# Reading the moving tile of a matmul from its two halves in turn, in a transformer block on one core

## The chip, the cores and the metric

The kernel runs on one core of a Trainium2 chip. The metric is the device time of one execution in microseconds, the median of several runs. Each kernel also has one profiled execution, from which all profile lines here come; its own time is given beside its span (first to last instruction of the program).

## The reference

One layer of a hybrid block on a sequence of 256 tokens of width 4096, all in float32. Cut to what matters, it is a chain of large products with attention-like work between them:

```python
h = _rmsnorm(x, norm_w[layer])
u = h @ w_in[layer]                                   # 4096 x 15424
... # split u: queries, keys, values and gates of an mLSTM (8 heads)
... # and of a sparse attention with three branches (16 heads)
y_ml = hm.reshape(B, S, ML_WIDTH) * jax.nn.sigmoid(ml_o) * jax.nn.silu(ml_z)
y_ns = _nsa(...) * jax.nn.silu(ns_z)
x = x + jnp.concatenate([y_ml, y_ns], axis=-1) @ w_out[layer]         # 4096 x 4096
x = x + jax.nn.sigmoid(x @ ple_gate[layer]) * (p[layer] @ ple_proj[layer])   # 4096 x 4096, 256 x 4096
```

The weights are some 400 MB of float32 and each is used once. With 256 tokens, each 128x512 piece of weights is multiplied by two stationary blocks of 128 tokens.

## The kernel before

**One product.** The activations are stationary (128 channels x 128 tokens, tiles `sh` and `sl`), the weights are the moving operand (128 channels x 512 output columns), and the result is a 128 x 512 accumulator in PSUM. To keep accuracy each float32 operand is split in a high and a low float32r part: ScalarE writes `whi` as a rounded copy of the loaded tile `raw` (line 1479), VectorE writes `wlo = raw - whi` (line 1480). A product is then three matmuls: high by high, low activations by high weights, high activations by low weights (function `product`, line 1234).

**Units.** The program is written out as a list of units. Each takes one tile `raw` of 128 x 2 x 512 (512 KB, one transfer from the SP queue), two blocks of 128 channels by 512 columns. `wide_group` (from line 894) makes eight groups of 16 units: each unit has 12 matmuls, on lines 913 and 915. `pair_group` makes all larger groups, 1024 columns each. Its plain units (`c_unit`) have 12 matmuls; its mixed units use a scheme with seven products in place of eight for a 2 x 2 arrangement of blocks, for which VectorE adds blocks of weights (function `sums`, lines 1277 to 1281) and of activations (tiles `cb`). All matmuls of `pair_group` are issued by `emit`, on line 1192. `p_unit` (lines 1373 to 1375) multiplies the small projection `ple_proj` in four of the groups.

Some products are not of this kind: `small_group` (lines 985, 986) has the weights as stationary operand and activations of 256 columns as the moving one, also float32r; `cmp_unit` (line 1005) takes plain float32 tiles; the two attentions (lines 539 to 631 and 707 to 733) multiply activations with activations.

**Order.** Engines work in the order that the loop at the end of `hymba_block` writes out. For each unit `n` it emits the split of unit `n + LOOK`, loads as long as fewer than six tiles are held, the unit's matmuls, and then a step of the other work (evictions, attention) from queues of generators:

```python
LOOK = 3
RAWB = 6
...
        if n + LOOK < N and not late:
            split(n + LOOK)
...
        load_some()
...
        un["mm"](*splits.pop(n))
```

So ScalarE and VectorE run up to three units ahead of TensorE, in four buffers each of `whi` and `wlo`.

**Layout.** The host function `_layout` lays the weights out so that each transfer is one contiguous piece of DRAM: `_blocks` for the groups of 512 columns and `ple_proj`, `_pairs` for the groups of 1024. In a tile, the 512 columns of a block are neighbours in a partition, 2 KB long.

Of the kernel before, what the change touches and what calls it, by code (L numbers as in the profile page):

```python
# [87 lines left out]
def hymba_block(ctx: ExitStack, tc: tile.TileContext, a, out: bass.AP):  # L88
    nc = tc.nc
    MM = nc.tensor.matmul  # L90
# [9 lines left out]
    def bank(bset, i, shape):  # L100
        if bset:
            return side(i, shape)
        return psp.tile(shape, F32, tag=f"mm{i // 2}", name=f"mm{i // 2}", bufs=2)
# [97 lines left out]
    def require(flag):  # L201
        n = 0
        while flag not in done:
            n += 1
            assert (step() or step_dry()) and n < 10000, flag
# [556 lines left out]
    sh, sl = [None] * 8, [None] * 8  # L762
# [125 lines left out]
    def gemm_unit(src, mm, pre=None, post=None, kind="wide"):  # L888
        units.append(dict(src=src, mm=mm, pre=pre, post=post, kind=kind))
# [4 lines left out]
    def wide_group(name, w, stat_flag, post, marks=None, after=None):  # L894

        flag = f"ev_{name}"
        box = {}
        prev = evq[-2] if len(evq) >= 2 else None
        evq.append(flag)

        def start():
            if prev:
                require(prev)
            box["ps"] = [bank(0, 2 - 2 * (SINGLES.index(name) % 2), [128, 512]) for _ in range(2)]

        for u in range(16):
            def mm(hi, lo, u=u):
                for j in range(2):
                    c, k = divmod(2 * u + j, 4)
                    first, last = (u == 0 and j == 0), (u == 15 and j == 1)  # L910
                    for s, m, st in ((sh, hi, first), (sl, hi, False)):
                        for t in range(2):
                            MM(box["ps"][t], s[c][:, k, t * 128:(t + 1) * 128], m[:, j, :], start=st, stop=False)  # L913
                    for t in range(2):
                        MM(box["ps"][t], sh[c][:, k, t * 128:(t + 1) * 128], lo[:, j, :], start=False, stop=last)  # L915

            def pre(u=u):
                if u == 0:
                    start()
                if stat_flag and u % 2 == 0:  # L920
                    require(f"{stat_flag}{u // 2}")

            def fin(u=u):
                if marks and u % 2:
                    done.add(f"{marks}{u // 2}")
                if u == 15:
                    post(box["ps"], flag)

            gemm_unit(w[u], mm, pre, fin)
            if after:  # L930
                after(u)
# [233 lines left out]
    def t_gate_own(g, own, us):  # L1165
# [9 lines left out]
        for j in range(2):  # L1175
# [11 lines left out]
                nc.vector.tensor_tensor(y[:, :, c0:c0 + 512], y[:, :, c0:c0 + 512], u, op=OP.mult)  # L1187
            yield

    def emit(seq):  # L1190
        for acc, s, m in seq:
            MM(acc.t, s, m, start=acc.i == 0, stop=acc.i == acc.n - 1)  # L1192
            acc.i += 1

    def pair_group(g, w, stat):
# [36 lines left out]
            return lambda k, t: (sh[c][:, b + k, t * 128:(t + 1) * 128], sl[c][:, b + k, t * 128:(t + 1) * 128])  # L1232

        def product(acc, st, hi, lo):
            return [(acc, st[0], hi), (acc, st[1], hi), (acc, st[0], lo)]

        def both(*products):
            emit([p for ps in zip(*products) for p in ps])
# [53 lines left out]
        def c_unit(kp, k, last):  # L1292
            split = split_and_sum

            def mm(hi, lo):
                bl = blocks(kp)
                if last:

                    tail.append((bl, k, hi, lo))
                    if len(tail) < (4 if g == 7 else 2):  # L1300
                        return
                    if g < -6:
                        for j in range(2):
                            for bl, k_, hi, lo in tail:
                                both(*(product(own[t][j], bl(k_, t), hi[:, j], lo[:, j]) for t in range(2)))
                        return
                    order = [(t, j) for j in range(2) for t in range(2)]
                    seq = [(b, i) for b in order[0:2] for i in range(3)] + [(b, 3) for b in order[0:2]]
                    for (t, j), i in seq + [(b, i) for b in order[2:4] for i in range(4)]:
                        bl, k_, hi, lo = tail[i]  # L1310
                        emit(product(own[t][j], bl(k_, t), hi[:, j], lo[:, j]))
                    return
                for j in range(2):
                    both(*(product(own[t][j], bl(k, t), hi[:, j], lo[:, j]) for t in range(2)))

            def post():
                if k:
                    finish(kp)
            unit(w[kp, k], split, mm, kp, post=post)

        def a_units(kp):
            def split1(r):
                raw[kp] = [r]
                return split_one(r)

            def split2(r):
                raw[kp].append(r)
                opened.extend(((kp, 0), (kp, 1)))
                return split_all(r, keep=True)

            def mm1(hi, lo):
                emit(product(oth[0], blocks(kp)(0, 0), hi[:, 0], lo[:, 0]))

            def mm2(hi, lo):
                both(product(own[0][0], mixed(kp, 2), hi[:, 0], lo[:, 0]),
                     product(own[0][1], blocks(kp)(1, 0), hi[:, 1], lo[:, 1]))
            unit(w[kp, 0], split1, mm1, kp, True)
            unit(w[kp, 1], split2, mm2, kp, True)
# [19 lines left out]
        def p_unit(j):  # L1358
            box = {}

            def pre():
                require("p")
                require(f"own{g - 1}")
                if g == 4:
                    require("r7")
                box["ps"] = [bank(1 - bset, 2 * j + t, [128, 512]) for t in range(2)]

            def mm(hi, lo):
                ps, ph, pl = box["ps"], held["ph"], held["pl"]
                for t in range(2):  # L1370
                    tk = slice(t * 128, (t + 1) * 128)
                    for k in range(2):
                        MM(ps[t], ph[:, k, tk], hi[:, k, :], start=(k == 0), stop=False)
                        MM(ps[t], pl[:, k, tk], hi[:, k, :], start=False, stop=False)
                        MM(ps[t], ph[:, k, tk], lo[:, k, :], start=False, stop=(k == 1))

            def t_pj():
                if j == 0:
                    pj[0] = wk.tile([128, 2, 2, 512], F32, tag="a", name="pj")
                for t in range(2):  # L1380
                    nc.scalar.activation(pj[0][:, j, t], box["ps"][t], AF.Copy)
                if j == 1:
                    done.add(f"pj{g}")
                yield
            units.append(dict(src=a["ple_proj"][2 * (g - 4) + 1 - j], mm=mm, pre=pre, post=lambda: urgent.append(t_pj()),
                              kind="pair", split=lambda r: split_all(r)))
# [90 lines left out]
    def split_all(r, keep=False):  # L1477
        hi, lo = split_tiles()
        nc.scalar.activation(hi, r, AF.Copy)  # L1479
        nc.vector.tensor_sub(lo, r, hi)  # L1480
        held_raw[0] -= not keep
        return hi, lo
# [100 lines left out]
    return o  # L1583


def _blocks(w, cols):

    k = w.shape[0]
    o = np.empty((len(cols), k // 256, 128, 2, 512), w.dtype)
    for g, c in enumerate(cols):  # L1590
        b = w[:, c:c + 512]
        o[g] = b.reshape(k // 256, 2, 128, 512).transpose(0, 2, 1, 3)
    return o


def _pairs(w):

    return np.ascontiguousarray(w.reshape(16, 2, 128, -1, 2, 512)[:, :, :, :, ::-1].transpose(3, 0, 1, 2, 4, 5))


def _layout(i):
# [7 lines left out]
        "x": c(x),  # L1609
        "xt": c(x.T.reshape(8, 4, 128, 256).transpose(0, 2, 1, 3)),  # L1610
        "w_in": _blocks(w_in, [COLS[n] for n in SINGLES]),
        "w_ip": _pairs(np.concatenate([w_in[:, COLS[n]:COLS[n] + 512] for p in PAIRS for n in p], 1)),
        "w_gate": _pairs(np.concatenate([w_in[:, GATE0[n] + 1024 * j:GATE0[n] + 1024 * j + 1024] for n, j in GATES], 1)),
        "w_out": _pairs(np.concatenate([i["w_out"][0][2048:], i["w_out"][0][:2048]])),
        "ple_gate": _pairs(i["ple_gate"][0]),
        "ple_proj": _blocks(i["ple_proj"][0], wide)[:, 0],
        "p": c(i["p"][0, 0].T.reshape(2, 128, 256).transpose(1, 0, 2)),
        "w_small": c(np.concatenate([w_in[:, 8192:8208], w_in[:, 13328:13376]], 1)
# [33 lines left out]
```

## Time and profile before

| | |
|---|---|
| median of 3 runs | 2119.56 us (2118.8 to 2121.72) |
| the profiled execution's own time | 2119.84 us |
| its span | 2117.8 us |
| TensorE busy with matmuls | 2103.6 us, 99% |
| TensorE weight loads | 1732.0 us, 82% (beside the matmuls) |
| VectorE busy | 1721.0 us, 81% |
| ScalarE busy | 1232.4 us, 58% |
| moved by transfers | 422.36 MB, mean 199 GB/s |
| granted TensorE clock | 0.999 |

How to read the profile: PE is TensorE's matmuls, PEld its weight loads, DVE VectorE, ACT ScalarE, POOL GpSimd, SP the queue that issues most transfers. A group's row has line, engine, operation, `out<-in` by the program's names, shapes, count, busy time, mean duration in ns of one, idle time before it and what ended it. Matmuls overlap one another, so that the duration of one (about 390 ns for 512 columns) is longer than the distance from one start to the next.

### The profile page before, as it was taken

What the parts mean: (1) busy time and instruction counts of PE and PEld (TensorE: products, weight loads), DVE (VectorE), ACT (ScalarE), POOL (GpSimd) and SP (SyncE); (2) the same over time, 40 slices, a digit from 0 to 9 for tenths busy, and PEclk for the clock granted to TensorE, in tenths of its full rate; (3) what the DMA queues carried; (4) which work ended last, traced back from release to release, by engine and by line L of the source; (5) the groups of instructions that cost most, each with busy time, mean ns of one, the idle gap of its engine ahead of it and who ended that gap; (6) DMA issues with size and microseconds to landing.
All of it is one profiled execution on the core that took longest, in us unless ns stands there. A gap on an engine that the chain in (4) does not pass through costs nothing.

```text
span 2117.8 us, 27056 instructions
## 1 busy us (share of the span) xinstructions
PE 2103.6 (99%) x9655; PEld 1732.0 (82%) x9655; DVE 1721.0 (81%) x2214; ACT 1232.4 (58%) x1621; POOL 42.5 (2%) x90
## 2 busy tenths in 40 slices
PE   9999999999999999999999999999999999999998
PEld 7877778888888888888888888888888888888887
DVE  7876699566666758959989999988998986988988
ACT  7684455565666464566555565665555555655554
POOL 1000000010000000000000000000000000000000
PEclk9999999999999999999999999999999999999999
DMA  9656665554444454745666567566665665556664
GB/s 362 227 170 212 243 210 198 210 182 155 150 152 146 166 170 152 242 153 189 208 207 211 191 207 231 182 204 244 210 206 197 210 220 169 203 201 227 203 215 145
DMA packets 118759, 422.36 MB, mean 199 GB/s; under 512 B 13906, under 2 KB 14474, under 8 KB 118624
## 3 DMA queue, kind: packets, MB, share of 16 engines
q1 hardware_dynamic: 114272, 409.00, 57.0%
q0 software_dynamic: 4208, 11.61, 1.8%
q8 instruction: 76, 1.25, 0.2%
q14 instruction: 59, 0.48, 0.1%
q10 hardware_dynamic: 144, 0.02, 0.0%
HBM read 416.08 MB, written 4.23 MB: 198 GB/s over the span
## 4 chain that ended last, share of the span: by engine, by line
PE 95%; DVE 3%; ACT 1%; DMA 1%; issue 1%; SPq 0%; ACTq 0%; DVEq 0%
PE mm L1192 43%; PE sd L1192 28%; PE mm L913 11%; PE mm L915 5%; DVE wlo L1480 2%; PE sd L628 1%; DMA raw<-in_w_ip 1%; PE sd L1005 1%; ACT whi L1479 1%; PE sd L818 1%; PE sd L279 1%; PE sd L615 0%; PE sd L631 0%; ACT xq L309 0%; PE sd L539 0%
## 5 line engine op out<-in xcount | busy, mean ns | idle before, releaser
L1479 ACT ACTIVATE whi<-raw 128x1024 fp32r<-128x1024 f32 x804 | 845.0, 1059 | 684.1 <-PE mm L1192 159.7
L1480 DVE TENSOR_TENSOR wlo<-raw,whi 128x1024 fp32r<-128x1024 f32 x804 | 976.2, 1222 | 278.8 <-ACT whi L1479 258.7
L1192 PE MATMUL mm<-whi,sh 128*128 128x512 f32 x1221 | 394.5, 393 | 1.7 <-DVE u L215 0.9
L1192 PE MATMUL mm<-wlo,sh 128*128 128x512 f32 x1221 | 390.1, 390 | 0.2
L1192 PE MATMUL mm<-whi,sl 128*128 128x512 f32 x1221 | 390.1, 390 | 0.0
L1192 PEld LDWEIGHTS mm<-whi,sh 128*128 128x128 f32 x1221 | 227.2, 188 | 51.6 <-issue 2.5
L1192 PEld LDWEIGHTS mm<-wlo,sh 128*128 128x128 f32 x1221 | 228.7, 188 | 49.4 <-DVE wlo L1480 2.2
L1192 PEld LDWEIGHTS mm<-whi,sl 128*128 128x128 f32 x1221 | 229.5, 188 | 48.4
L1192 PE MATMUL sd<-whi,sh 128*128 128x512 f32 x686 | 225.0, 390 | 0.0
L1192 PE MATMUL sd<-whi,sl 128*128 128x512 f32 x686 | 224.7, 389 | 0.0
L1192 PE MATMUL sd<-wlo,sh 128*128 128x512 f32 x686 | 224.7, 389 | 0.0
L913 PE MATMUL mm<-whi,sh 128*128 128x512 f32 x512 | 166.0, 405 | 0.0
L913 PE MATMUL mm<-whi,sl 128*128 128x512 f32 x512 | 158.3, 390 | 0.0
L915 PE MATMUL mm<-wlo,sh 128*128 128x512 f32 x512 | 158.0, 390 | 0.0
L1192 PEld LDWEIGHTS sd<-whi,sl 128*128 128x128 f32 x686 | 128.8, 188 | 26.8
L1192 PEld LDWEIGHTS sd<-wlo,sh 128*128 128x128 f32 x686 | 128.8, 188 | 26.7
L1192 PEld LDWEIGHTS sd<-whi,sh 128*128 128x128 f32 x686 | 128.5, 188 | 26.5
L1192 PE MATMUL sd<-whi,cb 128*128 128x512 f32 x450 | 145.9, 389 | 0.0
L1192 PE MATMUL mm<-whi,cb 128*128 128x512 f32 x390 | 130.0, 390 | 0.7 <-ACT whi L1479 0.7
L915 PEld LDWEIGHTS mm<-wlo,sh 128*128 128x128 f32 x512 | 96.1, 188 | 20.7
L913 PEld LDWEIGHTS mm<-whi,sl 128*128 128x128 f32 x512 | 96.1, 188 | 20.6
L913 PEld LDWEIGHTS mm<-whi,sh 128*128 128x128 f32 x512 | 92.7, 189 | 19.9 <-issue 3.8
(327 smaller groups left out, 2080.9 us busy)
## 6 DMA issues: line engine op xcount, KB each, us to landing
raw<-in_w_gate SPq DMA_DIRECT2D x192, 512.0 KB, 4.2
raw<-in_w_ip SPq DMA_DIRECT2D x159, 512.0 KB, 4.2
raw<-in_w_in SPq DMA_DIRECT2D x128, 512.0 KB, 3.5
raw<-in_w_out SPq DMA_DIRECT2D x128, 512.0 KB, 4.2
raw<-in_ple_gate SPq DMA_DIRECT2D x128, 512.0 KB, 3.5
raw<-in_w SPq DMA_DIRECT2D x16, 512.0 KB, 4.8
u<-in_xt SPq DMA_DIRECT2D x16, 256.0 KB, 7.7
xn<-in_x SPq DMA_DIRECT2D x4, 1024.0 KB, 6.1
```

The lines of the kernel that those rows point to most:

```text
L279: nc.tensor.transpose(p[:, i, :], u[:, t, i * 128:(i + 1) * 128], idn)
L628: MM(o[t][:, h, :], ptb[i][:, b, s, :], v[:, s, b, g * 128:(g + 1) * 128], start=(h == 0 and b == 0 and s == 0), stop=False)
L818: nc.tensor.transpose(pp[i // 2][:, i % 2, t * 128:(t + 1) * 128], src[:, t, k:k + 128], idn)
L913: MM(box["ps"][t], s[c][:, k, t * 128:(t + 1) * 128], m[:, j, :], start=st, stop=False)
L915: MM(box["ps"][t], sh[c][:, k, t * 128:(t + 1) * 128], lo[:, j, :], start=False, stop=last)
L1005: MM(o[64 * kv:64 * kv + 60], xq[l // 8][:, l % 8, 60 * kv:60 * kv + 60], raw[:, j, 256 * kv:256 * kv + 256], start=(l == 0), stop=(l == 31))
L1192: MM(acc.t, s, m, start=acc.i == 0, stop=acc.i == acc.n - 1)
L1479: nc.scalar.activation(hi, r, AF.Copy)
L1480: nc.vector.tensor_sub(lo, r, hi)
```

## The change

All products with weights as the moving operand read that operand in another order. A helper `paired` views the 512 columns of a block as two halves of 256 and goes through them in turn: element 0 of the first half, element 0 of the second, element 1 of the first, and so on. For the accumulators to hold the columns in the old order, the host puts even columns of a block in its first half and odd columns in its second (`_halves`, in `_blocks` and `_pairs`). The matmuls of `small_group`, `cmp_unit` and the attentions, and the layout of their operands, are as before.

```diff
@@ wide_group @@
-    MM(box["ps"][t], s[c][:, k, t * 128:(t + 1) * 128], m[:, j, :], start=st, stop=False)
+    MM(box["ps"][t], s[c][:, k, t * 128:(t + 1) * 128], paired(m[:, j]), start=st, stop=False)
...
-    MM(box["ps"][t], sh[c][:, k, t * 128:(t + 1) * 128], lo[:, j, :], start=False, stop=last)
+    MM(box["ps"][t], sh[c][:, k, t * 128:(t + 1) * 128], paired(lo[:, j]), start=False, stop=last)
@@ before emit @@
+    def paired(x):
+        return x.rearrange("p (b a) -> p a b", a=256)
@@ pair_group @@
     def product(acc, st, hi, lo):
+        hi, lo = paired(hi), paired(lo)
         return [(acc, st[0], hi), (acc, st[1], hi), (acc, st[0], lo)]
@@ p_unit @@
-    MM(ps[t], ph[:, k, tk], hi[:, k, :], start=(k == 0), stop=False)
-    MM(ps[t], pl[:, k, tk], hi[:, k, :], start=False, stop=False)
-    MM(ps[t], ph[:, k, tk], lo[:, k, :], start=False, stop=(k == 1))
+    MM(ps[t], ph[:, k, tk], paired(hi[:, k]), start=(k == 0), stop=False)
+    MM(ps[t], pl[:, k, tk], paired(hi[:, k]), start=False, stop=False)
+    MM(ps[t], ph[:, k, tk], paired(lo[:, k]), start=False, stop=(k == 1))
@@ host layout @@
+def _halves(w):
+    return w.reshape(*w.shape[:-1], 256, 2).swapaxes(-1, -2).reshape(w.shape)
...
-        o[g] = b.reshape(k // 256, 2, 128, 512).transpose(0, 2, 1, 3)
+        o[g] = _halves(b.reshape(k // 256, 2, 128, 512).transpose(0, 2, 1, 3))
...
-    return np.ascontiguousarray(w.reshape(16, 2, 128, -1, 2, 512)[:, :, :, :, ::-1].transpose(3, 0, 1, 2, 4, 5))
+    return _halves(w.reshape(16, 2, 128, -1, 2, 512)[:, :, :, :, ::-1].transpose(3, 0, 1, 2, 4, 5))
```

## The prediction

> **What bounds the kernel now.** I read the page first: shares of engines, then the chain that ended last.
>
> ```profile
> span 2117.8 us, 27056 instructions
> PE 2103.6 (99%) x9655; PEld 1732.0 (82%) x9655; DVE 1721.0 (81%) x2214; ACT 1232.4 (58%) x1621; POOL 42.5 (2%) x90
> PE 95%; DVE 3%; ACT 1%; DMA 1%; issue 1%; SPq 0%; ACTq 0%; DVEq 0%
> PE mm L1192 43%; PE sd L1192 28%; PE mm L913 11%; PE mm L915 5%; DVE wlo L1480 2%; PE sd L628 1%; DMA raw<-in_w_ip 1%; PE sd L1005 1%; ACT whi L1479 1%; PE sd L818 1%; PE sd L279 1%; PE sd L615 0%; PE sd L631 0%; ACT xq L309 0%; PE sd L539 0%
> ```
>
> TensorE is the bound, and 87% of the chain is matmuls of lines 1192, 913 and 915, the ones that the diff edits. What matters is the pace of one, from start to start, not its duration: matmuls overlap. The chain in order of time merges unbroken runs, and such a run divided by its count is the pace.
>
> ```profile
> 1047.52 6.80 PE sd L1192 x30
> 1067.01 11.11 PE sd L1192 x49
> 2100.32 11.12 PE sd L1192 x49
> ```
>
> 6.80 us over 30 is 226.7 ns, 11.11 over 49 is 226.7 and 11.12 over 49 is 226.9. It is one number from start to end. Does it depend on what else touches the memory? The same two places in the busy times by stretch (columns: PE, PEld, DVE, ACT, POOL, clock, DMA share, GB/s):
>
> ```profile
> 1067.10:1078.10 11.00, 11.00 (x50) 9.13 (x49) 8.91 (x12) 5.14 (x7) 0.00 (x0) 1.00 0.88 304
> 2100.40:2111.40 11.00, 11.00 (x49) 8.80 (x47) 9.06 (x13) 3.85 (x6) 0.00 (x0) 1.00 0.07 25
> ```
>
> The DMA share falls from 0.88 to 0.07 and the pace stays. So the pace is TensorE's own: granted clock 1.00, no transfer behind it. How far is it from what the array can do? The timeline has two other kinds of product to compare:
>
> ```profile
> 764.68 0.59 PE L731 MATMUL sd<-mv,pt 128*128 128x257 f32 x2
> 765.11 0.60 PE L732 MATMUL sd<-mv,pt 128*128 128x257 f32 x2
> 94.12 0.28 PE L985 MATMUL mm<-sh,whl 128*128 128x256 f32 x1
> 94.23 0.28 PE L986 MATMUL mm<-sl,whl 128*128 128x256 f32 x1
> 94.95 0.28 PE L986 MATMUL mm<-sl,whl 128*128 128x256 f32 x1
> ```
>
> Lines 731 and 732 take plain float32 tiles. Two of them start in 765.11 - 764.68 = 0.43 us, so one takes 215 ns for 257 columns: 0.837 ns a column. The weight products (float32r) take 226.7 / 512 = 0.443 ns a column, a little more than half of that. If a plain column is two steps, a step is 215 / 514 = 0.418 ns, and 512 steps would be 214 ns, say 215 with rounding. A weight product takes 11.7 ns more, 5.4%. The float32r products of 256 columns (lines 985, 986) tell whether this excess goes with the columns: the first starts 0.11 us before the second, where 256 x 0.418 is 0.107 and 256 x 0.443 is 0.113. Later ones come at (94.95 - 94.23) / 6 = 0.12, perhaps held by the weight loads, of which each has one. That fits an excess by column, without proving it: a stall in the reading of the moving tile, which at float32r takes 4 bytes a step, twice the rate of the plain products that show no such excess.
>
> **The change part by part.** Nothing is added or removed: same instructions, stationary operands, waits, issues and bytes. `paired` alters the address order of the moving tile in lines 913, 915, 1192 and 1373 to 1375: from 512 neighbours to elements 0, 256, 1, 257, and so on, one from each half, 1 KB apart. `_halves` permutes the columns in DRAM on the host, so the results come out in the old order and every consumer of an accumulator is as before.
>
> The splits (lines 1479, 1480) and the sums of halves of weight blocks (lines 1277 to 1281) work element by element on whole 512-column blocks that are all permuted alike; they read contiguously still. I cost them at nothing, and the transfers too: a tile is one contiguous piece in DRAM as before. There is no cover that could go away. The narrow products (lines 985, 986) and the plain ones of line 1005 are not edited.
>
> What is left is the pace, times the count:
>
> ```profile
> L1192 PE MATMUL mm<-whi,sh 128*128 128x512 f32 x1221 | 394.5, 393 | 1.7 <-DVE u L215 0.9
> L913 PE MATMUL mm<-whi,sh 128*128 128x512 f32 x512 | 166.0, 405 | 0.0
> L913 PE MATMUL mm<-whi,sl 128*128 128x512 f32 x512 | 158.3, 390 | 0.0
> L915 PE MATMUL mm<-wlo,sh 128*128 128x512 f32 x512 | 158.0, 390 | 0.0
> L1373 PE MATMUL sd<-whi,ph 128*128 128x512 f32 x16 | 6.2, 389 | 0.0
> L1375 PE MATMUL mm<-wlo,ph 128*128 128x512 f32 x16 | 6.2, 389 | 0.0
> 0.00:990.00 990.00, 511.03 (x2199) 410.44 (x2200) 1.00 0.57 194
> 990.00:2118.00 1128.00, 1089.80 (x4784) 895.79 (x4782) 1.00 0.61 204
> ```
>
> The last two rows are line 1192 by stretch (first count: matmuls, one or two that straddle the cut counted twice): 2199 + 4782 = 6981. With 3 x 512 of lines 913 and 915, and six groups of 16 of lines 1373 to 1375 (first and last shown), 8613 products are edited: 3735 before 990 us, 4878 after. At 226.7 ns they are 1952 us of the 2117.8.
>
> The trace shows no matmul whose moving tile is read in this order, so the new pace is bounded from both sides. Below: 215 ns, the step of lines 731 and 732; 11.7 ns less, 8613 x 0.0117 = 101 us gross. Above: 429 ns, if one read is served for each 0.837 ns, as the plain products need at most: 202 ns more. Between them lies 226.7. A nearer row is line 580, whose moving operand (kh, columns 0 to 127 of two branches) is two runs of 128 that lie 1 KB apart:
>
> ```profile
> 460.02 0.28 PE L580 MATMUL sd<-kh,qh 128*128 128x256 f32 x1
> 460.14 0.28 PE L581 MATMUL sd<-kh,ql 128*128 128x256 f32 x1
> 460.25 0.28 PE L582 MATMUL sd<-kl,qh 128*128 128x256 f32 x1
> ```
>
> It starts its follower 0.11 to 0.12 us later, as the contiguous lines 985 and 986 do: a jump of 1 KB inside an operand costs nothing by itself. I take the lower end, 215 ns. My reason is where the excess sits: it is there only when the moving tile is fetched at full rate from one advancing place, and half that rate (plain float32) shows none. In the new order each of two places advances at half the rate. That is an inference; no row shows it.
>
> [...]
>
> **What the gain meets.** Not all of it comes out, because VectorE makes the split tiles:
>
> ```profile
> 990.00:2010.00 1020.00, 1020.00 (x4562) 844.38 (x4561) 907.47 (x1057) 586.93 (x653) 6.35 (x9) 1.00 0.61 206
> DVE wlo L1480 <- ACT whi L1479: 258.7, 226, 4.1
> ACT whi L1479 <- PE mm L1192: 159.7, 154, 3.0
> PE sd L1192 <- DVE wlo L1480: 2.4, 5, 0.8
> ```
>
> After 990 us VectorE is busy 907 of 1020 us, 89%, and TensorE never idles. Today's VectorE idle time goes largely back to TensorE (a split waits for a tile that a matmul frees), so part of it shrinks with the pace. At full gain the stretch would be 1020 - 4562 x 0.0117 = 967 us (some 95% are edited, so nearer 969), and VectorE 94% busy, with only three units split ahead. I expect bursts of evictions and block sums to hold TensorE there, and count 60% of the gain of that part: 4878 x 11.7 x 0.6 = 34 us. Before 990 us I count all: 3735 x 11.7 = 44 us. Sum: 78 us. The profiled execution took 2119.84 us, 0.28 above the median of the runs, so against either: 2119.84 - 78 = **2042 us**.
>
> **The rivals.**
>
> *VectorE takes all of it in the second half.* If its 112 us of idle time there (1020 - 907) are needed whole, as latencies between engines and not as waits for TensorE, only the 44 us before 990 come out: 2076 us. For: 89% busy, few tiles ahead. Against: the wait for ScalarE traces back to TensorE.
>
> *The order of reads doesn't matter.* Then the 11.7 ns belong to float32r itself (array passes, weight swap): 2119.8 us. For: a fixed 13 ns a product would give the 0.12 us of lines 985 and 986 as well. Against: their first interval of 0.11.
>
> *The stall doubles.* If each of the two places brings the stall that one brings now, in its turn, each product costs 11.7 ns more: 2119.8 + 101 = 2221 us. Nothing speaks for it but that no row excludes it.
>
> *Each read goes to another place and is served alone.* This is the slower side. Strided reads elsewhere in the kernel pay by element:
>
> ```profile
> L309 ACT ACTIVATE xq<-ct,pe_c 128x60 f32<-128x60 f32 x64 | 20.2, 387 | 0.0
> L598 ACT ACTIVATE s<-s,mx 128x256 f32<-128x256 f32 x32 | 16.1, 503 | 9.9 <-DVE mx L593 9.8
> L598 ACT ACTIVATE s<-s,mx 128x128 f32<-128x128 f32 x32 | 12.5, 392 | 5.8 <-DVE mx L593 5.8
> L547 DVE TENSOR_TENSOR sc<-sd,biasc x8: 246/252/258, 462.3 to 660.8; 128x60 f32<-128x60 f32 x8
> L799 DVE TENSOR_TENSOR s<-s 128x256 f32<-128x256 f32 x25 | 10.5, 418 | 0.0
> L800 DVE TENSOR_TENSOR s<-s 128x128 f32<-128x128 f32 x25 | 7.3, 292 | 0.9
> ```
>
> Line 309 reads every 16th element (64 bytes apart). Contiguous ScalarE work goes by (503 - 392) / 128 = 0.87 ns an element, so 60 elements should take 392 - 68 x 0.87 = 333 ns; it takes 387, 0.9 ns more an element. Line 547 has the same step in one VectorE operand: 292 - 68 x 0.98 = 225 against 252, 0.45 more. With TensorE's nearest price, 0.837 ns a read, a product takes 429 ns and the kernel 2119.8 + 8613 x 0.202 = 3860 us; with the 0.45 to 0.9 of the other engines added to each element it would be 4100 to 6100. It decides as soon as a read that leaves its neighbour costs more than the 0.443 ns a column has now. Against: those rows never come back to a place, while here each place is used by every second read, and line 580's jump is free.
>
> [...]
>
> **How the numbers follow.** Gain with part held by VectorE, 2042 us: 0.42. VectorE takes the second half, 2076: 0.10. No difference, 2119.8: 0.20. Stall doubled, 2221: 0.08. Each read served alone, 3860 or more: 0.20. A measurement of this kernel tells about 0.2% (4 us) from no change. So faster 0.52, same 0.20, slower 0.28. The range leaves out only the last case, 0.20: from 2015, all of the gross gain and the rounding of the pace (2119.8 - 101 = 2019), to 2225. The forecast's own range is 2015 to 2095; within cases of both signs it is this that I mean by 2042.
>
> **What would show it.** Right: runs of 30 products in the chain take 6.45 us in place of 6.80, the 256-column products of lines 985 and 986 stay at 0.12, VectorE's share rises above 90% in the stretch after the first half, and TensorE shows idle time that ends with line 1480's split. VectorE as bound: the same pace in runs, but idle time of TensorE of some 25 us or more. No difference: 6.80 again. Stall doubled: about 7.15. Reads served alone: near 12.9, TensorE still at 99%, VectorE's share halved. Wrong altogether would be a changed duration of the splits, or of transfers, which I cost at nothing.

## The result

The changed kernel takes 2041.69 us (median of 4 runs, 2041.1 to 2042.32) against 2120.24 us before (2118.8 to 2121.72 in 4 runs): a ratio of 0.9629, 95% interval 0.9613 to 0.9646. Its profiled execution took 2042.32 us with a span of 2040.3 us, 77.5 us less than the span before.

The page of the changed kernel (line 1192 is now 1195, the splits of lines 1479 and 1480 are 1483 and 1484):

```profile
span 2040.3 us, 27056 instructions
PE 2013.5 (99%) x9655; PEld 1741.4 (85%) x9655; DVE 1713.6 (84%) x2214; ACT 1221.5 (60%) x1621; POOL 42.5 (2%) x90
PE 89%; DVE 7%; issue 2%; ACT 1%; DMA 1%; SPq 0%; DVEq 0%; ACTq 0%
L1484 DVE TENSOR_TENSOR wlo<-raw,whi 128x1024 fp32r<-128x1024 f32 x804 | 973.2, 1220 | 224.9 <-ACT whi L1483 217.2
```

The instructions are the same in number, and a split takes 1220 ns as before (1222). In the chain TensorE has given up 6 points, and VectorE went from 3% to 7%. The pace stands in the chain in order of time, in the same kind of runs as before:

```profile
1047.15 6.47 PE mm L1195 x30
1109.81 10.58 PE mm L1195 x49
2023.32 10.59 PE sd L1195 x49
```

Two narrow products, which the change leaves alone, in the timeline:

```profile
90.38 0.28 PE L985 MATMUL mm<-sh,whl 128*128 128x256 f32 x1
90.50 0.28 PE L986 MATMUL mm<-sl,whl 128*128 128x256 f32 x1
```

6.47 / 30 = 215.7 and 10.58 / 49 = 215.9 ns a product, where it was 226.7; the narrow ones still start 0.12 us apart. Over undisturbed intervals the pace is 215.8 to 215.9 ns, so 8613 products should gain 8613 x 10.8 ns = 93 us. The profiled execution gained 77.5. The other 15.5 us were lost on the way. To see where, cut the changed kernel at its 3735th edited product, as the kernel before was cut at 990 us. The cut lies at 956.6 us (line 1195 by stretch):

```profile
0.00:956.60 956.60, 488.53 (x2199) 412.64 (x2200) 1.00 0.59 201
956.60:2040.30 1083.70, 1040.67 (x4783) 900.57 (x4782) 1.00 0.63 212
```

All engines in the stretch that answers to 990 to 2010 before, with the same 4562 matmuls and 1057 VectorE instructions (PE, PEld, DVE, ACT, POOL, clock, DMA share, GB/s). The row under it is a short stretch of the first part:

```profile
956.60:1937.50 980.90, 975.15 (x4562) 848.91 (x4562) 902.54 (x1057) 580.12 (x653) 6.35 (x9) 1.00 0.63 214
197.30:200.70 3.40, 3.40 (x12) 2.13 (x9) 2.31 (x3) 1.80 (x2) 0.00 (x0) 0.50 0.64 202
```

And TensorE's waits for the splits (in total us, times, longest):

```profile
PE sd L1195 <- DVE wlo L1484: 8.0, 15, 0.9
PE mm L1195 <- DVE wlo L1484: 4.0, 8, 0.9
```

The first part took 990.1 us and takes 956.6: 33.5 gained of 3735 x 10.8 = 40.3. The second took 1127.7 and takes 1083.7: 44.0 of 52.7. So 6.8 us are lost in the first part and 8.7 in the second. In the stretch of the second, VectorE's busy time is nearly what it was, 902.5 us for 907.5, now of 980.9 (92%, before 89%), and TensorE, which had no idle time there, has 5.8 us. TensorE's waits for a split, 2.4 us before, are 12.0. A wait in this list begins only when the matmul before has ended; since a matmul lasts some 380 ns and the next starts after 216, a shorter delay isn't in it, so that the real loss can be larger. One part of the loss isn't a stall: from 197.3 us on the clock was granted at half for 3.4 us, while in the kernel before it is 1.00 up to the last 5 us. By the starts of the same matmuls in both traces that costs some 1.5 of the 6.8 us.

### The profile page after: what moved, and what is told of

It is laid out like the page before. It is cut to its first block, busy times and chain, and to the rows that moved or that the text cites. A ratio compares the mean times of both kernels' runs of the same rounds, so it can differ in the third digit from the quotient of the medians.

```text
span 2040.3 us, 27056 instructions
## 1 busy us (share of the span) xinstructions
PE 2013.5 (99%) x9655; PEld 1741.4 (85%) x9655; DVE 1713.6 (84%) x2214; ACT 1221.5 (60%) x1621; POOL 42.5 (2%) x90
## 3 DMA queue, kind: packets, MB, share of 16 engines
q1 hardware_dynamic: 114272, 409.00, 59.0%
## 4 chain that ended last, share of the span: by engine, by line
PE 89%; DVE 7%; issue 2%; ACT 1%; DMA 1%; SPq 0%; DVEq 0%; ACTq 0%
PE mm L1195 40%; PE sd L1195 26%; PE mm L913 10%; PE mm L915 5%; DVE wlo L1484 4%; PE sd L628 1%; PE sd L1005 1%; ACT whi L1483 1%; DMA raw<-in_w_ip 1%; PE sd L818 1%; PE sd L279 1%; PE sd L615 1%; DVE raw L1281 1%; DVE raw L1284 0%; ACT xq L309 0%
## 5 line engine op out<-in xcount | busy, mean ns | idle before, releaser
L1484 DVE TENSOR_TENSOR wlo<-raw,whi 128x1024 fp32r<-128x1024 f32 x804 | 973.2, 1220 | 224.9 <-ACT whi L1483 217.2
L1195 PE MATMUL mm<-whi,sh 128*128 128x512 f32 x1221 | 381.1, 383 | 3.0 <-DVE u L215 1.7
L1195 PE MATMUL mm<-wlo,sh 128*128 128x512 f32 x1221 | 377.9, 380 | 1.9 <-DVE wlo L1484 1.6
L1195 PE MATMUL mm<-whi,sl 128*128 128x512 f32 x1221 | 377.1, 379 | 0.0
L1195 PE MATMUL sd<-whi,sh 128*128 128x512 f32 x686 | 217.9, 379 | 0.0
L1195 PE MATMUL sd<-wlo,sh 128*128 128x512 f32 x686 | 217.8, 379 | 0.0
L1195 PE MATMUL sd<-whi,sl 128*128 128x512 f32 x686 | 217.6, 379 | 0.0
L913 PE MATMUL mm<-whi,sh 128*128 128x512 f32 x512 | 159.9, 394 | 0.0
L915 PE MATMUL mm<-wlo,sh 128*128 128x512 f32 x512 | 152.3, 379 | 0.0
L913 PE MATMUL mm<-whi,sl 128*128 128x512 f32 x512 | 152.2, 379 | 0.0
L1195 PE MATMUL sd<-whi,cb 128*128 128x512 f32 x450 | 141.2, 379 | 0.0
```

The lines of the kernel that those rows point to most:

```text
L913: MM(box["ps"][t], s[c][:, k, t * 128:(t + 1) * 128], paired(m[:, j]), start=st, stop=False)
L915: MM(box["ps"][t], sh[c][:, k, t * 128:(t + 1) * 128], paired(lo[:, j]), start=False, stop=last)
```

## The experiments

### Which orders are fast

Stretches of 24 matmuls were put behind the last unit of the kernel before, where little else runs. The edits of these stretches are shown shortened. Each reads one float32r tile (`r`, 512 columns) with a 128 x 128 stationary block, and the results go nowhere.

```diff
+    for o, s, m in run("flat", st[:, 0:128], r, 24):
+        MM(o, s, m, start=True, stop=True)
...
+    ... run("halves", st[:, 0:128], r.rearrange("p (b a) -> p a b", a=256), 24)
+    ... run("quarters", st[:, 0:128], r.rearrange("p (b a) -> p a b", a=128), 24)
+    ... alt(a): r.rearrange("p (c b a) -> p c a b", b=2, a=a)        # a = 64, 16, 8, 4, 2
+    ... step b: r.rearrange("p (a b) -> p b a", b=b)                 # b = 2, 4, 16
```

> The kernel before, with 14 stretches of 24 float32r matmuls (512 columns, 128 x 128 stationary) put behind its last unit, each stretch reading one tile in another order; their results go nowhere. Pace from start to start. Theory A (two reads in a row from one small piece of the memory collide; any order that leaves the piece at each read is free of it): flat 226.7 ns; halves, quarters, tiles and step16 216 ns; the alternations get slow again below the size of the piece, so alt64 and alt16 216, alt4 and alt2 227. Theory B (two readers, one for even and one for odd reads, each of which wants neighbours): flat 227, halves, tiles, alt64 and alt16 216; quarters and step16, where each reader jumps at every read, 430 or more. Rival C (the order of reads isn't it, the gain comes from the kernel's schedule): all stretches the same, 227.

The chain in order of time (start, length, count; alt with 64, 16, 8, 4 and 2 elements are lines 1593 to 1601, steps of 2, 4 and 16 elements lines 1603 to 1607, two blocks of the tile in turn, 2 KB apart, line 1609):

```profile
2121.66 5.44 PE flat L1587 x24
2127.10 5.18 PE halves L1589 x24
2132.28 6.79 PE quarters L1591 x24
2139.07 5.18 PE alt L1593 x24
2154.61 5.18 PE alt L1599 x24
2159.79 5.47 PE alt L1601 x24
2165.26 10.87 PE step L1603 x24
2176.13 11.07 PE step L1605 x24
2187.20 10.40 PE step L1607 x24
2197.60 5.18 PE tiles L1609 x24
```

Flat is 226.7 ns and halves 215.8, the numbers of the two kernels. So the order of reads alone does it, and rival C falls. Alternation is as good at every distance from 2 KB (tiles) down to four elements, 16 bytes (215.8), and no better than flat at two elements (227.9). Four places in turn are slow, 282.8. And each of the three plain steps is slow: 433 ns for every 16th element, 461 for every 4th, 452 for every 2nd. Theory A promised 216 for step 16 and for quarters, so it falls too. Theory B comes closest, though its 430 for quarters is far from 283.

### What else could make the excess: stationary width, columns, plain float32

```diff
+    ... run("flat64", st[:, 0:64], r), run("flat32", st[:, 0:32], r)
+    ... run("n384", st[:, 0:32], r[:, 0:384]), run("n256", st[:, 0:32], r[:, 0:256])
+    ... run("h256", st[:, 0:32], r[:, 0:256].rearrange("p (b a) -> p a b", a=128))
+    ... run("plain", idn, pf[:, 0], 8), "phalves" and "pstep16" in the same way     # float32
```

> As the run of the orders, with other stretches: flat reading with stationary tiles of 128, 64 and 32 columns, with 512, 384 and 256 moving columns, and plain float32 tiles (8 products each, two instructions a product). If the weight loads take the 11 ns from the moving stream (rival D), flat64 has about half the excess (221 ns) and flat32 a quarter (218.5); if the moving stream makes it alone (theories A and B), all stay at 227. If the excess goes by column, n256 with 32 stationary columns is 113 and n384 170 ns; if it is fixed to a matmul, 120 and 173. h256 (two halves of 128) is 109 if halves cure it. Plain float32: 429 ns an instruction flat, the same in halves; step16 the same if a lone read costs at most 0.837 ns, and up to twice that if jumps cost as on ScalarE.

Lines 1587, 1589 and 1591 are flat with 128, 64 and 32 stationary columns:

```profile
2122.31 5.44 PE flat L1587 x24
2127.75 5.52 PE flat L1589 x24
2133.27 5.56 PE flat L1591 x24
2144.01 4.16 PE n L1595 x24
2148.17 2.83 PE n L1597 x24
2150.99 2.62 PE h L1599 x24
2156.49 6.87 PE plain L1603 x16
2163.36 8.64 PE phalves L1605 x16
2172.00 13.72 PE pstep L1607 x16
```

Narrower weight loads don't lower the pace: 226.7, 230.0, 231.7. Rival D, the weight loads, falls. 384 columns take 173.4 ns (line 1595) and 256 take 117.8 (line 1597), both with 32 stationary columns: the excess doesn't shrink with the columns, as one by column would (170 and 113). 256 columns in halves take 109.1 (line 1599), so narrow products could gain too. Plain float32 is 429 ns an instruction; here halves cost 540, where the same 429 was expected, and every 16th element 857. Of these two types float32r alone gains, and the same edit on plain float32 would be a loss.

### A theory of two readers

From these two runs I formed theory B2, a guess at what would give these times: that the reads go alternately to two readers, and that the pace goes by how many reads in a row each finds in the same 16 bytes. Flat would give each reader every other element, two reads out of each 16 bytes (227 ns); halves, or alternation by 16 bytes or more, would give it four (216 ns). A further set of stretches was made to separate that from one reader.

```diff
+    ... run("pairs", st[:, 0:128], r.rearrange("p (b c a) -> p c b a", b=2, a=2))    # 0 1 256 257 2 3 ...
+    ... run("twice", st[:, 0:128], r[:, 0:256, None].to_broadcast([128, 256, 2]))    # 0 0 1 1 2 2 ...
+    ... "fourfold", "reverse", "eighths" (eight places), "q32" (four places, 16 bytes apart), "plaintwice"
```

> The kernel before with further orders behind its last unit, 24 float32r matmuls each. Theory B2, made from the run of the orders: reads 1, 3, 5 ... and reads 2, 4, 6 ... go to two readers, each fetches 16 bytes at a time, and the pace goes by how many reads in a row a reader finds in its 16 bytes: 4 (halves, alternation by 16 bytes or more) 216 ns, 2 (flat) 227, 1 (every second, fourth or sixteenth element) 430 to 460, two pieces in turn (quarters) 283. It gives: pairs (two elements of one half, two of the other) 283, twice (each element two times) and fourfold 216, reverse 227, q32 (four places 16 bytes apart in turn) 283 or less, eighths (four places in turn for each reader) 430; plaintwice (float32) 429. Theory A (one reader; a jump at least at every second read is what helps): pairs 216, twice and fourfold 227, q32 216 or 283. Mixed: flat and halves in turn, 226.7 and 215.8 in turn if each pays for itself.

```profile
2134.35 8.15 PE pairs L1591 x24
2142.50 5.18 PE twice L1593 x24
2147.68 5.18 PE fourfold L1595 x24
2152.86 5.61 PE reverse L1597 x24
2158.47 11.74 PE eighths L1599 x24
2170.21 6.44 PE q L1601 x24
2176.65 6.87 PE plaintwice L1603 x16
```

Twice is the telling one. It reads 256 neighbours, each two times, without any jump, and is as fast as halves (216 ns): counted for two readers, each of them gets four reads out of 16 bytes. One reader could be helped by that too, but then halves, which leave the place at every read (215.8), could not be fast. Pairs jumps between the halves at every second read, which in B2's count is alternating places for each reader: 339 ns, where theory A had 216. It also answers a rival that neither theory has, one reader that keeps two pieces of 16 bytes at hand: in every eight reads pairs and halves touch the same eight elements, so that for one such reader they would cost the same, and they cost 339 and 216 ns. Only which of them fall on odd and which on even reads differs. The readers themselves remain a guess; no run shows them. B2 tells fast from slow in all these cases. Its sizes are only roughly right: pairs 339 for 283, eighths 489 for 430, reverse 233.5 for 227. In the mixed stretch, flat and halves in turn, a flat matmul was followed after 0.23 us and one in halves after 0.21 to 0.22; 22 pairs took 9.83 us, 447 ns each, 4 ns above the 442.5 of a flat one and one in halves among their like. So the cost stays with the flat ones.

### By column or by matmul

```diff
+    ... run("cols448", st[:, 0:128], r[:, 0:448]), and 512, 384, 320; "half384", "half448"
+    ... run("blocks", st[:, 0:128], r.rearrange("p (b c a) -> p c b a", b=2, a=4))   # 0-3 256-259 4-7 ...
+    ... run("later", st[:, 0:128], r[:, 2:512]), run("four", st[:, 0:128], r[:, 4:512])
```

> The kernel before with further stretches of 24 float32r matmuls behind its last unit, stationary 128 x 128. Flat reading of 512, 448, 384 and 320 columns: if the excess is fixed to a matmul, 226.7, 200.0, 173.3 and 146.7 ns; if it goes by column (the prediction's reading), 226.7, 198.3, 170.0 and 141.7. In halves, 384 columns 162.5 and 448 columns 189.2. blocks (four neighbours of one half, four of the other): each of the two readers finds two reads in 16 bytes, so 227 to 234 by theory B2; 216 if it is enough to leave a place at times. later (510 columns from the third on) and four (508 from the fifth on): 226 and 225 if the start of the tile doesn't matter.

Lines 1591, 1593 and 1595 are flat with 448, 384 and 320 columns, 1597 and 1599 halves of 384 and 448:

```profile
2131.34 4.86 PE cols L1591 x24
2136.21 4.19 PE cols L1593 x24
2140.39 3.51 PE cols L1595 x24
2143.91 3.90 PE half L1597 x24
2147.81 4.54 PE half L1599 x24
2152.35 5.62 PE later L1601 x24
2157.97 5.44 PE four L1603 x24
2163.41 5.99 PE blocks L1605 x24
```

In halves, 384 and 448 columns take 162.4 and 189.2 ns; with the 215.8 for 512 that is 0.417 ns a column and 2.3 ns for the matmul. Flat ones take 146.3, 174.6, 202.7 and 226.7 ns for 320, 384, 448 and 512 columns, which is 12.9, 14.5, 15.9 and 13.2 above 0.417 a column: near enough fixed to the matmul, not in proportion. A tile that begins 8 bytes later pays 22 ns (later: 234.4 for 510 columns), one that begins 16 bytes later 15 (four: 226.7 for 508). blocks is 250, and B2 said 227 to 234: blocks and flat both give a reader two reads in a row by its count, but the order that changes place after them (250) costs more than the one that goes on to the next 16 bytes (flat, 227). So "reads in a row out of 16 bytes" doesn't give all the times. Nor does it say why flat, with two such reads, keeps close to 0.417 ns a column from 320 to 512 columns and pays a nearly fixed 13 to 16 ns for each matmul instead; no run settles why.

One more observation bears on it. After a pause of TensorE (3.57 us, until ScalarE's line 1571), the first stretch of the first set began at half clock (timeline):

```profile
2114.07 1.05 PE L1585 MATMUL lead<-whi,sh 128*128 128x512 f32 x2
2115.36 1.05 PE L1585 MATMUL lead<-whi,sh 128*128 128x512 f32 x2
```

The same line by stretch, with the granted clock 0.50 after the two busy times:

```profile
2114.00:2116.50 2.50, 2.50 (x7) 1.94 (x6) 0.50 0.18 62
```

Three flat matmuls took 1.29 us there by the rounded times, 430 ns each to within 3 ns. In the changed kernel's stretch of granted clock 0.50 two products in halves took 0.85 us (line 1195, starts at 199.37 and 200.22 us), 425 to within 5. So at half clock flat reading shows no excess over halves beyond the rounding, where a proportional one would make it 453. There a column takes 0.84 ns; in plain float32 it takes as long (0.837 ns), and there too flat (429) isn't slower than halves (540). No run shows why flat pays its excess only where a column takes 0.42 ns.

### The order of reads in the full kernel

Two variants of the changed kernel, with the columns in DRAM laid to match: neighbouring pieces of four elements in turn, and four places in turn.

```diff
-        return x.rearrange("p (b a) -> p a b", a=256)
+        return x.rearrange("p (c b a) -> p c a b", b=2, a=4)      # fours
+        return x.rearrange("p (b a) -> p a b", a=128)             # quarters
```

> The changed kernel with alternation between neighbouring pieces of four elements (0, 4, 1, 5, 2, 6, 3, 7, 8, 12 ...) in place of the halves; the columns in DRAM lie to match. By theory B2 the distance of the two places doesn't matter from 16 bytes on: 215.9 ns a product and 2041 to 2042.5 us. If the halves are needed for another reason in the full kernel (other engines write the same tile's neighbours), up to 2119.

> The changed kernel with four places in turn (0, 128, 256, 384, 1, 129 ...), the columns in DRAM laid to match. If the order of reads alone sets the time, as the stretch of quarters behind the kernel had it (283 ns a product), 2119.3 + 8613 x (282.8 - 226.7) ns = 2602 us, TensorE still busy 99% and waiting for nobody. If the kernel's gain came from something that any interleaving has (the layout in DRAM, the writes of the splits), it stays near 2042.

Fours took 2042.67 us (ratio to the kernel before 0.9634, 0.9620 to 0.9648), the changed kernel's time. Quarters took 2591.53 us (ratio 1.2226, 1.2190 to 1.2262), 0.4% below the 2602 expected. The page of quarters and a run of its chain:

```profile
PE 2579.5 (100%) x9655; PEld 1766.0 (68%) x9655; DVE 1736.6 (67%) x2214; ACT 1251.0 (48%) x1621; POOL 42.4 (2%) x90
1065.31 24.08 PE mm L1195 x85
```

24.08 / 85 = 283.3 ns, as in the stretch. The same kind of change, two places more in turn, makes the kernel 22% slower in place of 3.7% faster.

### Only the groups of 512 columns

```diff
         def product(acc, st, hi, lo):
-            hi, lo = paired(hi), paired(lo)
...
-    return _halves(w.reshape(16, 2, 128, -1, 2, 512)[:, :, :, :, ::-1].transpose(3, 0, 1, 2, 4, 5))
+    return np.ascontiguousarray(w.reshape(16, 2, 128, -1, 2, 512)[:, :, :, :, ::-1].transpose(3, 0, 1, 2, 4, 5))
```

> Only the eight groups of 512 columns and the small projection read in halves (1536 + 96 products); the pair groups as before. If VectorE holds only the pair groups, all of the gain comes out: 1632 x 10.8 ns = 17.6 us, 2101.5 us against 2119.1. If it holds everything alike (83% came out in the whole), 2104.5.

It took 2099.84 us against 2119.28 (ratio 0.9906, 0.9891 to 0.9920): 19.4 us, all of the 17.6 expected, and no less by VectorE. The 1.8 above lie within the interval (3 us).

### What held the other 15 us

The additions of weight blocks (`sums`) were left out in both kernels, 289 us of VectorE.

```diff
         def sums(kp, k):
+            return
```

> The changed kernel without the additions of weight blocks (function sums, 420 VectorE additions of 0.69 us, 289 us): the mixed products then use blocks that aren't sums; all matmuls, splits and transfers stay. If the 15 us that the kernel lost of 8613 x 10.8 = 93 us are VectorE's bursts, the time falls to 2027 to 2033 us; if VectorE doesn't hold TensorE, it stays at 2040 to 2042.

> The kernel before without the same additions: 2114 to 2120 us by either theory, since TensorE hardly waits for VectorE there. The difference to the changed kernel without them should then be the pure gain of the pace, 93 us, if VectorE held the rest.

The changed kernel fell to 2021.41 us (2020.01 to 2022.47), by 20.3, some 6 us below the lowest time expected; the kernel before fell to 2113.99 (2113.07 to 2115.15), by 5.1. The page's shares for the changed kernel without them:

```profile
PE 2006.3 (99%) x9655; PEld 1745.4 (86%) x9655; DVE 1459.7 (72%) x1794; ACT 1225.6 (61%) x1621; POOL 42.4 (2%) x90
```

And for the kernel before without them:

```profile
PE 2101.0 (99%) x9655; PEld 1734.4 (82%) x9655; DVE 1463.7 (69%) x1794; ACT 1236.8 (59%) x1621; POOL 42.4 (2%) x90
```

Between the two lie 92.6 us, the pure gain of the pace (93). With the additions it is 78.6 by the medians. So the missing 14 us hang on the additions. In the changed kernel without them, the list of TensorE's waits has none for a split; with them it had 12.0 us. Not shown is in which of two ways they cost it: by the 289 us of VectorE, or because ScalarE's copies of the summed blocks have to wait for them (250.7 us in the changed kernel, lines 1282 and 1285). Leaving the additions out removes both.

### Two tries to get them back

One mixed product in each of 14 groups was made plain:

```diff
+PLANS = {g: [("C", k) if (kind, k) == ("a", 7) else (kind, k) for kind, k in p if (kind, k) != ("c", 7)]
+         for g, p in PLANS.items()}
```

> The changed kernel with one mixed product (number 7) made plain in 14 of the 20 pair groups: 42 matmuls more (+9.1 us of TensorE), some 66 us less of VectorE. If VectorE's bursts cost 15 us, 2038 to 2046 us; if they cost nothing, 2050.8.

2047.11 us (ratio to the kernel before 0.9657, 0.9642 to 0.9671), between the two expectations: of the 9.1 us of matmuls that it added, 3.7 came back, with an interval of some 3 us. VectorE's additions fell from 420 to 364, 13%, and 13% of the 20.3 us that all of them cost is 2.7. So the work taken away returned about its share, and these 14 mixed products save more in matmuls than they cost in additions.

Half of the additions were moved to GpSimd:

```diff
             else:
-                nc.vector.tensor_add(r[:, 0], r[:, 0], r0[:, 1])
-                nc.vector.tensor_add(r[:, 1], r[:, 1], r[:, 0])
+                nc.gpsimd.tensor_add(r[:, 0], r[:, 0], r0[:, 1])
+                nc.gpsimd.tensor_add(r[:, 1], r[:, 1], r[:, 0])
```

> The changed kernel with half of the additions of weight blocks (210 of 420, those of the second half of each mixed block) on GpSimd in place of VectorE. Without all 420 it took 2021.4 us. If GpSimd needs about 1 us each and they come in time, 2028 to 2035; if its additions come late or hold VectorE up, above 2042.

2163.67 us (ratio 1.0209, 1.0192 to 1.0226), slower than the kernel before. Two of its groups of instructions:

```profile
L1284 POOL TENSOR_TENSOR raw<-raw 128x512 f32<-128x512 f32 x105 | 219.4, 2089 | 1095.5 <-DVE raw L1282 851.2 <-ACT whi L1483 226.3 <-issue 18.1
L1484 DVE TENSOR_TENSOR wlo<-raw,whi 128x1024 fp32r<-128x1024 f32 x804 | 1064.2, 1339 | 366.7 <-ACT whi L1483 359.1 <-PE mm L1195 0.9
```

And ScalarE's longest wait:

```profile
ACT whi L1483 <- POOL raw L1285: 322.6, 101, 3.5
```

An addition takes 2.07 to 2.09 us there, not the 1 us that I assumed (VectorE: 0.69), and VectorE's splits rise from 1220 to 1339 ns on average. ScalarE waits 323 us for the sums, and TensorE for ScalarE (58.5 us, before the move 2.8). The mean granted clock of its profiled execution was 0.995 (the changed kernel's 0.998), and 0.005 of 2160.6 us is 11 us, at most so much of the 122 us that this kernel takes above the changed one. Neither of these versions beats the changed kernel.

## Why the prediction was right, and where its steps were not

**What bounds the kernel** held: TensorE's pace, independent of transfers. Quarters, in which TensorE waits for no split, moved as 8613 times its pace to 0.4%, and without the additions so did the change itself (92.6 of 93 us).

**Nothing but the order of reads counts**, in the part by part costing, held: a split takes 1220 ns (1222 before), an addition 683 to 692 (684 to 692), the transfers move 409.00 MB on the main queue in both, and the narrow products start 0.12 us apart.

**The new pace** was taken as 215 ns and is 215.8. The term of the sum is 93 us, not 101: the lower bound was read from plain float32 rows rounded to 10 ns, which by the starts in the trace come every 216 to 217 (764.68 to 765.98 us, 1.30 us for the six of lines 731 to 733). A matmul in halves takes 2.3 ns more than its 512 columns at 0.417.

**"An excess by column"** was wrong. It was read from one interval of 0.11 us at line 985; the flat stretches of 320 to 512 columns show 13 to 16 ns a matmul. The later 0.12 us, which the prediction put down to the weight loads, was the truer reading: behind the kernel 256 flat columns take 120.0 ns with 128 stationary columns and 117.8 with 32. That step didn't enter the sum, since all edited products have 512 columns. It did serve to turn down the rival "the order of reads doesn't matter", whose argument, a fixed 13 ns, was true and still didn't make the rival true.

**"Each of two places advances at half the rate"** pointed the right way for a reason that is only half right. Two places of the tile aren't what matters: twice is as fast (216 ns) and has one place, and step 16 leaves its place at every read and takes 433 ns. What sorts the times is B2's count, of how many reads in a row of every second one lie in the same 16 bytes: 216 with four or more, 227 to 234 with two (250 in blocks), 268 to 489 with one. What in the chip makes it so, no run shows.

**What the gain meets** was right in kind: of the evictions and block sums that the prediction named, the sums are enough, as the runs without them show. The split was wrong. I let 23 us be lost, all after 990 us. Of the 93 us, 6.8 are lost in the first part and 8.7 in the second. The sum, 78 us, came out right because 8 us too much gross gain met 7 us too much loss; that it lies so near the measured 77.5 is luck. VectorE's share in the stretch after the first part rose above 90%, as forecast, but to 92% and not 94%.

**The rivals.** VectorE taking all of the second half: 44 us came out there, where it gave none. No difference: excluded by the interval. The doubled stall: not seen. Each read served alone: the plain steps of 2, 4 and 16 elements pay about what it was priced at, 433 to 461 ns against 429; the order of this change, which also leaves its place at every read, doesn't (215.8). Nor is leaving the place at every read what the slow ones share: a step of 2 elements reads each 16 bytes twice in a row and takes 452 ns.

## What to carry to other kernels

If float32r matmuls follow one another at about 227 ns for 512 columns, reading the moving tile in turn from two places at least 16 bytes apart, each advancing by neighbours, brought them to 216 here, provided that the columns can be laid to match at no cost; on plain float32 the same edit loses a quarter (429 to 540). Try the order in a short stretch behind the kernel first: four places cost 18 to 25% over flat, steps of 2, 4 or 16 elements 91 to 103%. And when the bound engine gets 5% faster, ask what the next one does in that stage: with VectorE at 89% a sixth of the gain was lost, and nearly as much in the first part, where it was busy 73% on average. The average alone doesn't show where it is short.

## What the runs showed of the hardware

Unexpected was that every second element (452 ns) is slower than flat (227) and no faster than every 16th (433), that 512 reads of 256 elements, each twice, take less than 512 reads of neighbours (216 against 227 ns), that flat reading has no excess over halves at half clock (430 against 425 ns, to the rounding), and that a tile begun 8 bytes later pays 22 ns in place of 13. Narrower stationary blocks made flat reading slower, 231.7 ns with 32 columns against 226.7 with 128; no run here explains that.
